# Order of TensorE in a two-layer decoder trunk: narrow instructions take turns with wide products

## The chip, the cores and the metric

The kernel runs on one core of a Trainium2 chip. The metric is the device time of one execution, in microseconds; a row of the profile is one instruction, or a run of equal ones, of that execution. Besides the engine for products (TensorE, PE in the rows, with its loads of weights shown apart as PEld) the core has VectorE (DVE), ScalarE (ACT), GpSimd (POOL) and SyncE (SP, which issues the transfers).

## The reference, cut to what matters

A trunk of two layers on x (512 tokens, width 1024). Layer 0 mixes by a gated delta rule (4 heads of 128) and by dilated window attention (8 heads of 64), layer 1 by a diagonal state-space model (S5) and a gated product; each layer then attends into 256 memory tokens and runs a SwiGLU of hidden width 2816. All in float32.

```python
def reference(x, mem, positions, ...):
    h = x
    for layer in range(DEPTH):
        i = layer // 2
        if layer % 2 == 0:
            mix = delta_dilated_mixer(h, positions, hyb_w_in[i], ..., hyb_w_out[i])
        else:
            mix = s5_mixer(h, s5_a_re[i], ..., s5_glu_wo[i], s5_glu_wg[i])
        h = post_norm(h, mix, ln_mix_g[layer], ln_mix_b[layer])
        h = post_norm(h, memory_cross_attention(h, mem, ...), ln_x_g[layer], ln_x_b[layer])
        h = post_norm(h, swiglu(h, ffn_wg[layer], ffn_wu[layer], ffn_wd[layer]), ...)
    return h

    # inside the delta rule: chunks in order, each needs the state of the one before
    def step(state, inp):
        q_c, w_c, u_c, k_c, a_c, gl = inp
        v_new = u_c - einsum(w_c, state)
        out = einsum(q_c, state) + einsum(a_c, v_new)
        state = state * exp(gl) + einsum(k_c, v_new)
        return state, out
```

## The kernel before

**Products.** Every float32 product with weights is made from three: both operands are split into a high and a low part (tiles `hi` and `lo`, made by ScalarE and VectorE from `raw`, into which the weights are loaded), and high times high, high times low and low times high are added up in one bank of the accumulator (`ps`, 8 banks). Such a product moves 512 or 256 columns past a 128x128 tile of weights; these are called *wide* below. The *narrow* instructions are transposes (128x128, `ident` in the row) and products of unsplit float32 tiles: 128x128 in the delta rule, 64x64 and 32x32 in the inverse of its triangular matrices.

**Recording and planning.** The program doesn't issue as it goes. Each operation is recorded by the class `Order` with its cost (`cost`) and its predecessors; its number in the record (moved a little for weights and tables) is its priority. `Order.order` then simulates the engines. Whenever an engine is free it takes the ready operation with the lowest number whose tiles can be had, looking past at most `TRIES` (40) others. The cost of each operation and fixed delays between engines set when the next is ready, so the plan of one engine depends on the costs of all. `issue` writes the instructions out in the order found, each engine's own queue in program order; hence nearly all rows carry one line, L439 (several instructions recorded as one: L437). Since the plan fills an engine's gaps with what is ready, wide products of the next part of the program are found between the steps of a chain.

**The first mixer, where the prediction looks.** In the order of the record: the input projection of the delta rule with its convolution; on VectorE the solve of 31 triangular rows (tiles `big_119` and `t2_184`, two operations a row, the next row needing the one before); the gate of z (`z_sink`, which writes `big_68` from `t2_205` to `t2_208`); the solved rows go out to memory and come back, are masked (`t2_210` to `t2_216`, by `masks`), transposed (into `ps_211` to `ps_217`, **T287** below, after the second number in `ps_211_287`), and inverses are put together from 32x32 and 64x64 pieces (banks `ps_218` to `ps_233`). Then the delta rule, four chunks of 128 tokens in a chain. A step is called by the second number of its bank: F316 and F318 (state and output of the first chunk), **F325** (the key times the state), F327, F333, **T324** (transposes of the chunk's output), **F329** and F331 (the next state), F339, F341, F347, T338, F343, and so on to **T402**, transposes for the attention. Between two products of this chain VectorE or ScalarE read the bank and write the next operand. The wide products that fill are the projections for the attention: V into `ps_292` and `ps_293`, and the keys or queries for the rotation into `ps_308_384` and `ps_309_385` (24 wide products each). Behind that come the window attention, its output product (`ps_612` and others), whose operands are transposed first (`ps_627`, `ps_628`), cross-attention and the FFN.

Of the kernel before, what the change touches and what calls it, by code (L numbers as in the profile page):

```python
# [33 lines left out]
TRIES = 40  # L34
FILL = 1
PRE = 1
GATE = 5
STEPS = (4, 2)
LATER = 100
FFN_PARTS = ((0, 6), (6, 11))  # L40
# [64 lines left out]
class Order:  # L105
# [173 lines left out]
    def scratch(self, ap):  # L279
        self.hist.setdefault(ap.tensor.name, ([], []))  # L280


    def order(self, seq, prio):
        ops = self.ops
# [35 lines left out]
        sched = [False] * n  # L320
        dma_free = 0.0
        slow = 3.4
        out = []
        for op in ops:
            if npred[op.i] == 0:
# [2 lines left out]
        while len(out) < n:  # L328
# [5 lines left out]
            for e in self.eng:  # L334
                if busy[e] > now + 1e-9:
                    nxt.append(busy[e])
                    continue
                skipped, got = [], None
                tries = 0
                while heaps[e]:  # L340
                    item = heapq.heappop(heaps[e])
                    op = ops[item[1]]
                    if sched[op.i]:
                        continue
                    ok = True
                    need = {}
                    for t in op.tiles:
                        if t in live or t not in self.tags:
                            continue
                        tag, b = self.tags[t]  # L350
                        need[tag] = need.get(tag, 0) + 1
                        if sum(x <= now + 1e-9 for x in free[tag]) < need[tag]:
                            if free[tag]:
                                nxt.append(min(free[tag]))
                            ok = False
                            break
                        f = first[t]
                        if tag in KEEP and len(free[tag]) <= KEEP[tag][0] and rank[t] > rank_at[tag][head] + KEEP[tag][1]:
                            ok = False
                            break  # L360
                        if f > head and prof[tag][head:f].max(initial=0) >= b:
                            ok = False
                            break
                    if ok:
                        got = op
                        break
                    skipped.append(item)
                    tries += 1
                    if tries > TRIES:
                        break  # L370
                for it in skipped:
                    heapq.heappush(heaps[e], it)
                if got is None:
                    continue
                op = got
                a = next(x for x in op.alts if x[0] == e)
                for t in op.tiles:
                    if t in self.tags and t not in live:
                        tag, b = self.tags[t]
                        live.add(t)  # L380
                        free[tag].sort()
                        free[tag].pop(0)
                        if first[t] > head:
                            prof[tag][head:first[t]] += 1
                sched[op.i] = True
                op.engine = e
                op.start = now
                if e == "sp":
                    busy[e] = now + a[4]
                    nbytes = max(_bytes(x) for x in op.outs + op.ins)  # L390
                    s = max(now + 1.65, dma_free)
                    dma_free = s + nbytes / 3.6e5
                    op.done = dma_free + 0.75
                else:
                    cost = a[4]
                    if e == "pe":
                        if now - busy[e] > 3.4:
                            slow = now + 3.4
                        cost += min(cost, max(slow - now, 0.0) * 0.5)
                    busy[e] = now + cost  # L400
                    op.done = busy[e]
                nxt.append(busy[e])
                out.append((op, a))
                for t in op.tiles:
                    if t in self.tags:
                        end[t] = max(end.get(t, 0.0), op.done)
                        left[t] -= 1
                        if left[t] == 0:
                            tag, b = self.tags[t]
                            free[tag].append(end[t] + self.LAT)  # L410
                            prof[tag][head:last[t] + 1] -= 1
                for s in op.succ:
                    npred[s.i] -= 1
                    when[s.i] = max(when[s.i], op.done + self.LATS.get((e, s.alts[0][0]), self.LAT))
                    if npred[s.i] == 0:
                        heapq.heappush(pend, (when[s.i], s.i))
                while head < n and sched[seq[head].i]:
                    head += 1
# [23 lines left out]
def _size(ap):  # L442
    n = 1
    for _, c in list(ap.ap)[1:]:
        n *= c
    return n
# [1268 lines left out]
```

## Time and profile before

| | us |
|---|---|
| runs of the kernel | 1540.59, 1544.35, 1544.91 |
| median | 1544.35 |
| the profiled execution | 1543.56 |
| span of its records | 1541.8 |
| TensorE busy within the span | 1508.7 |
| VectorE, ScalarE, GpSimd busy | 984.9, 552.5, 57.0 |

The profile shows one execution. The span runs from the first record to the last; 1.8 us of the execution lie around it. A timeline row tells when a run of equal instructions started and how long it lasted; matmuls overlap, so what one costs is read from the start of one row to the start of the next. In brackets stands the time in which the engine had nothing to do just before, and the engine whose result ended it.

### The profile page before, as it was taken

Reading aid. Unit: us, or ns where it says so; the run is one execution under the profiler, and the core shown is the slowest. Engines: PE = TensorE matmul, PEld = TensorE weight load, DVE = VectorE, ACT = ScalarE, POOL = GpSimd, SP = SyncE. Lnnn points to the kernel's source line nnn. Section 1 sums busy time; section 2 is a strip of 40 time slices with the busy share of each in tenths; the row PEclk is TensorE's granted clock in tenths of the full one; section 3 lists DMA queues with packets and bytes.
Section 4 is the critical chain, followed back from the end, with each engine's and each line's share of the span. In section 5 each row is a group of like instructions: output and inputs, shape, how many; then the busy total and the mean of one; then the engine's idle time right before and its main releaser. Section 6 shows DMA issues by size and latency. Waiting matters only on the chain.

```text
span 1541.8 us, 21120 instructions
## 1 busy us (share of the span) xinstructions
PE 1508.7 (98%) x8220; PEld 1268.3 (82%) x8220; DVE 984.9 (64%) x1880; ACT 552.5 (36%) x1008; POOL 57.0 (4%) x97
## 2 busy tenths in 40 slices
PE   7999899999999999999999899999999999999998
PEld 5888788689889887888888898888889888888886
DVE  6986576697557888626845899647557444234436
ACT  5533346544523354324341333323423222122311
POOL 1100000010100000010000000000000000000000
PEclk9999999999999999999999999999999999999999
DMA  6424134235223355445562652333212333233322
GB/s 201 115 57 123 47 119 137 64 98 163 62 76 116 110 192 176 150 165 174 186 220 76 245 191 86 128 110 121 65 57 82 109 99 102 85 110 96 96 69 96
DMA packets 125396, 184.01 MB, mean 119 GB/s; under 512 B 14128, under 2 KB 84656, under 8 KB 121200
## 3 DMA queue, kind: packets, MB, share of 16 engines
q1 hardware_dynamic: 125296, 182.66, 37.6%
q8 instruction: 65, 1.06, 0.3%
q14 instruction: 35, 0.29, 0.1%
HBM read 162.45 MB, written 20.19 MB: 118 GB/s over the span
## 4 chain that ended last, share of the span: by engine, by line
PE 88%; DVE 7%; DMA 2%; ACT 1%; issue 1%; SPq 0%; POOL 0%; DVEq 0%; ACTq 0%; POOLq 0%
PE ps L439 86%; DVE t L439 4%; DVE big L439 2%; PE ps L437 2%; DVE lo L439 1%; DMA raw<-in_hyb_w_in_dram 1%; DVE tiny L439 0%; DMA big<-s5m 0%; ACT big L439 0%; DMA raw<-in_xo_w_dram 0%; ACT hi L439 0%; ACT t L439 0%; DMA posi<-in_pos_t_dram 0%; SPq L439 0%; ACT L439 0%
## 5 line engine op out<-in xcount | busy, mean ns | idle before, releaser
L439 PE MATMUL ps<-big,hi 128*128 128x512 f32 (+1 forms) x2368 | 649.5, 360 | 6.1 <-ACT hi L439 4.5
L439 PE MATMUL ps<-hi,big 128*128 128x512 f32 x1728 | 548.2, 394 | 0.7 <-ACT big L439 0.4
L439 PEld LDWEIGHTS ps<-big,hi 128*128 128x128 f32 x2368 | 420.7, 190 | 72.4 <-ACT hi L439 4.7
L439 ACT ACTIVATE hi<-raw 128x1024 fp32r<-128x1024 f32 (+2 forms) x252 | 263.5, 1046 | 513.7 <-PE ps L439 355.7
L439 DVE TENSOR_TENSOR lo<-raw,hi 128x1024 fp32r<-128x1024 f32 (+2 forms) x252 | 303.4, 1205 | 224.8 <-ACT hi L439 221.4
L439 PE MATMUL ps<-big,lo 128*128 128x512 f32 (+1 forms) x1184 | 423.7, 359 | 2.5 <-DVE lo L439 2.5
L439 PEld LDWEIGHTS ps<-hi,big 128*128 128x128 f32 x1728 | 322.6, 188 | 66.4 <-DVE big L439 0.9
L439 PE MATMUL ps<-lo,big 128*128 128x512 f32 x864 | 338.3, 393 | 1.0 <-DVE lo L439 1.0
L439 PEld LDWEIGHTS ps<-big,lo 128*128 128x128 f32 x1184 | 224.6, 190 | 34.5 <-DVE lo L439 2.9
L439 PEld LDWEIGHTS ps<-lo,big 128*128 128x128 f32 x864 | 162.4, 188 | 35.5 <-DVE lo L439 2.2
L439 ACT ACTIVATE big<-ps 128x256 fp32r<-128x256 f32 (+2 forms) x188 | 89.4, 508 | 211.1 <-PE ps L439 202.0
L439 ACT ACTIVATE t<-ps 128x512 f32<-128x512 f32 (+6 forms) x147 | 68.8, 485 | 147.7 <-PE ps L439 139.0
L439 DVE TENSOR_TENSOR big<-ps,big 128x256 fp32r<-128x256 f32 (+1 forms) x152 | 77.6, 541 | 56.9 <-ACT big L439 54.7
L439 DVE SCALAR_TENSOR_TENSOR big<-big,ps 128x512 f32<-128x512 f32 x56 | 38.4, 685 | 86.7 <-PE ps L439 86.7
L439 DVE SCALAR_TENSOR_TENSOR t<-t,ps 128x512 f32<-128x512 f32 x72 | 49.0, 682 | 68.5 <-ACT t L439 49.8
L439 ACT ACTIVATE big<-t 32x128 f32<-32x128 f32 (+2 forms) x148 | 64.9, 455 | 24.3 <-DVE t L439 19.9
L439 DVE SCALAR_TENSOR_TENSOR big<-big,tiny,t 128x512 f32<-128x512 f32 x96 | 66.6, 745 | 0.0
L439 PE MATMUL ps<-ident,t 128*128 128x128 f32 x344 | 62.7, 275 | 3.4 <-ACT t L439 1.8
L439 POOL TENSOR_TENSOR tiny<-tiny,mhalf 128x1 f32<-128x1 f32 (+1 forms) x28 | 23.1, 825 | 962.3 <-DVE tiny L439 953.6
L439 PEld LDWEIGHTS ps<-ident,t 128*128 128x128 f32 x344 | 42.5, 140 | 15.6 <-ACT t L439 5.1
L439 PE MATMUL ps<-big,big 128*128 128x256 f32 (+2 forms) x328 | 54.9, 314 | 0.0
L439 PEld LDWEIGHTS ps<-big,big 128*128 128x128 f32 x328 | 47.8, 190 | 5.0
(145 smaller groups left out, 929.4 us busy)
## 6 DMA issues: line engine op xcount, KB each, us to landing
raw<-in_ffn_wg_dram SPq DMA_DIRECT2D x44, 512.0 KB, 3.8
raw<-in_ffn_wu_dram SPq DMA_DIRECT2D x44, 512.0 KB, 3.6
raw<-in_ffn_wd_dram SPq DMA_DIRECT2D x44, 512.0 KB, 4.1
s5m<-big SPq DMA_DIRECT2D x16, 1024.0 KB, 4.2
big<-s5m SPq DMA_DIRECT2D x16, 1024.0 KB, 6.3
raw<-in_hyb_w_in_dram SPq DMA_DIRECT2D x26, 512.0 KB, 3.8
raw<-in_xk_w_dram SPq DMA_DIRECT2D x16, 512.0 KB, 3.6
raw<-in_xv_w_dram SPq DMA_DIRECT2D x16, 512.0 KB, 4.1
```

Source lines behind the costliest of these rows:

```text
L437: op.inst = getattr(self.eng[e], f)(*a, **k)
L439: op.inst = getattr(self.eng[e], fn)(*args, **kw)
```

## The change

The planner gets two numbers, `WIDE` and `REACH`, and a function that sorts TensorE's operations into narrow and wide ones. When the last operation planned for TensorE was narrow, another narrow one that is ready is passed over in favour of a wide one that is ready and recorded at most 100 behind the first narrow one passed over; up to 200 operations are looked past for that. If there is none, the narrow one is taken as before. In the planner's account a narrow operation right behind a wide one costs 0.08 us less. No instruction is added or removed on any engine; since the plan's times change, VectorE, ScalarE and SyncE are written in another order too.

```diff
--- before.py
+++ after.py
@@ -35,6 +35,8 @@
 FILL = 1
 PRE = 1
 GATE = 5
+WIDE = 200
+REACH = 100
 STEPS = (4, 2)
 LATER = 100
 FFN_PARTS = ((0, 6), (6, 11))
@@ -279,6 +281,16 @@
     def scratch(self, ap):
         self.hist.setdefault(ap.tensor.name, ([], []))
 
+    @staticmethod
+    def kind(op):
+
+        _, fn, args, kw, _ = op.alts[0]
+        if fn == "transpose":
+            return "narrow"
+        if fn == "matmul":
+            return "wide" if args[1].dtype == F32R and _size(op.outs[0]) >= 256 else "narrow"
+        return fn
+
 
     def order(self, seq, prio):
         ops = self.ops
@@ -320,6 +332,7 @@
         sched = [False] * n
         dma_free = 0.0
         slow = 3.4
+        after = None
         out = []
         for op in ops:
             if npred[op.i] == 0:
@@ -335,7 +348,7 @@
                 if busy[e] > now + 1e-9:
                     nxt.append(busy[e])
                     continue
-                skipped, got = [], None
+                skipped, got, narrow = [], None, None
                 tries = 0
                 while heaps[e]:
                     item = heapq.heappop(heaps[e])
@@ -361,15 +374,19 @@
                         if f > head and prof[tag][head:f].max(initial=0) >= b:
                             ok = False
                             break
+                    if ok and e == "pe" and after == "narrow" and (self.kind(op) != "wide" or narrow is not None and prio[op.i] > prio[narrow.i] + REACH):
+                        narrow = narrow or op
+                        ok = False
                     if ok:
                         got = op
                         break
                     skipped.append(item)
                     tries += 1
-                    if tries > TRIES:
+                    if tries > (TRIES if narrow is None else WIDE):
                         break
                 for it in skipped:
                     heapq.heappush(heaps[e], it)
+                got = got or narrow
                 if got is None:
                     continue
                 op = got
@@ -394,6 +411,10 @@
                 else:
                     cost = a[4]
                     if e == "pe":
+                        kind = self.kind(op)
+                        if kind == "narrow" and after == "wide":
+                            cost -= 0.08
+                        after = kind
                         if now - busy[e] > 3.4:
                             slow = now + 3.4
                         cost += min(cost, max(slow - now, 0.0) * 0.5)
```

The first place is on TensorE, in front of the output product of the first mixer (`ps_612`), where its operands are transposed (`ident`). Before:

```order
L439 MATMUL ps_612_688<-hi_618_694,big_235_311 128x512
L439 MATMUL ps_627_703<-ident_1_72,big_580_656 128x128 x4
L439 MATMUL ps_612_688<-hi_618_694,big_235_311 128x512
L439 MATMUL ps_628_704<-ident_1_72,big_580_656 128x128 x4
L439 MATMUL ps_612_688<-lo_619_695,big_235_311 128x512
```

and now:

```order
L460 MATMUL ps_612_688<-lo_616_692,big_234_310 128x512
L460 MATMUL ps_627_703<-ident_1_72,big_580_656 128x128
L460 MATMUL ps_612_688<-hi_615_691,big_234_310 128x512
L460 MATMUL ps_627_703<-ident_1_72,big_580_656 128x128
L460 MATMUL ps_612_688<-hi_618_694,big_235_311 128x512
L460 MATMUL ps_627_703<-ident_1_72,big_580_656 128x128
L460 MATMUL ps_612_688<-lo_619_695,big_235_311 128x512
L460 MATMUL ps_627_703<-ident_1_72,big_580_656 128x128
```

The four transposes into one bank stood together; now a wide product stands between each two.

The second place is on TensorE, where the delta chain begins (transposes into `ps_211`, from the masked rows `t2_210`). Before:

```order
L439 MATMUL ps_293_369<-lo_305_381,big_9_80 128x512
L439 MATMUL ps_293_369<-hi_304_380,big_9_80 128x512
L439 MATMUL ps_308_384<-hi_313_389,big_6_77 128x512
L439 MATMUL ps_308_384<-lo_314_390,big_6_77 128x512
L439 MATMUL ps_308_384<-hi_313_389,big_6_77 128x512 x2
L439 MATMUL ps_211_287<-ident_1_72,t2_210_286 128x128 x4
L439 MATMUL ps_213_289<-ident_1_72,t2_212_288 128x128 x4
L437 MATMUL ps_218_294<-t2_210_286,big_98_172 32x32 x8
```

and now:

```order
L460 MATMUL ps_308_384<-hi_316_392,big_7_78 128x512 x2
L460 MATMUL ps_308_384<-lo_317_393,big_7_78 128x512
L460 MATMUL ps_308_384<-hi_316_392,big_7_78 128x512
L460 MATMUL ps_309_385<-hi_313_389,big_6_77 128x512
L460 MATMUL ps_309_385<-lo_314_390,big_6_77 128x512
L460 MATMUL ps_309_385<-hi_313_389,big_6_77 128x512 x2
L460 MATMUL ps_309_385<-lo_314_390,big_6_77 128x512
L460 MATMUL ps_309_385<-hi_313_389,big_6_77 128x512
L460 MATMUL ps_211_287<-ident_1_72,t2_210_286 128x128 x4
L458 MATMUL ps_218_294<-t2_210_286,big_98_172 32x32 x8
```

Before, four wide products into `ps_308` (an x2 counts two) stand between the last one into `ps_293` and these transposes; now twelve into `ps_308` and six into `ps_309` do, of which the last twelve are shown. VectorE, whose triangular solve must end before, reads there, around the last gate of z (`t2_208`), before:

```order
L439 SCALAR_TENSOR_TENSOR t2_208_284<-t2_208_284,ps_192_268 128x512
L439 TENSOR_TENSOR big_119_195<-big_119_195,t2_184_260 64x13x19
L439 SCALAR_TENSOR_TENSOR big_68_142<-t2_208_284,normg_29_101 128x512
L439 TENSOR_TENSOR t2_184_260<-big_119_195 64x240
L439 TENSOR_TENSOR big_119_195<-big_119_195,t2_184_260 64x12x20
```

and now:

```order
L460 SCALAR_TENSOR_TENSOR t2_208_284<-t2_208_284,ps_192_268 128x512
L460 TENSOR_TENSOR big_119_195<-big_119_195,t2_184_260 64x17x15
L460 SCALAR_TENSOR_TENSOR big_68_142<-t2_208_284,normg_29_101 128x512
L460 TENSOR_TENSOR t2_184_260<-big_119_195 64x256
L460 TENSOR_TENSOR big_119_195<-big_119_195,t2_184_260 64x16x16
```

The gate stood behind the row of 13 by 19 and now stands ahead of the row of 16 by 16: eight operations more of the solve come behind it.

The third place is on TensorE in the delta chain, from F327 (`ps_251`) to F329 (`ps_253`). Before:

```order
L439 MATMUL ps_248_324<-ident_1_72,t2_247_323 128x128
L439 MATMUL ps_309_385<-hi_319_395,big_8_79 128x512
L439 MATMUL ps_248_324<-ident_1_72,t2_247_323 128x128
L439 MATMUL ps_309_385<-lo_320_396,big_8_79 128x512
L439 MATMUL ps_248_324<-ident_1_72,t2_247_323 128x128 x2
L439 MATMUL ps_309_385<-hi_319_395,big_8_79 128x512 x2
L439 MATMUL ps_309_385<-lo_320_396,big_8_79 128x512
L439 MATMUL ps_309_385<-hi_319_395,big_8_79 128x512
L439 MATMUL ps_309_385<-hi_322_398,big_9_80 128x512
L439 MATMUL ps_309_385<-lo_323_399,big_9_80 128x512
L439 MATMUL ps_309_385<-hi_322_398,big_9_80 128x512
L439 MATMUL ps_253_329<-t2_252_328,big_25_97 128x128 x4
```

and now:

```order
L460 MATMUL ps_240_316<-t2_239_315,big_25_97 128x128 x4
L460 MATMUL ps_242_318<-t2_239_315,big_99_173 128x128 x4
L460 MATMUL ps_309_385<-lo_323_399,big_9_80 128x512
L460 MATMUL ps_249_325<-t2_241_317,big_66_140 128x128 x4
L460 MATMUL ps_309_385<-hi_322_398,big_9_80 128x512
L460 MATMUL ps_251_327<-t2_250_326,big_119_195 128x128 x4
L460 MATMUL ps_257_333<-t2_241_317,big_65_139 128x128 x4
L460 MATMUL ps_248_324<-ident_1_72,t2_247_323 128x128 x4
L460 MATMUL ps_253_329<-t2_252_328,big_25_97 128x128 x4
L460 MATMUL ps_255_331<-t2_252_328,big_99_173 128x128 x4
```

The wide products into `ps_309` between the steps are gone but for two, and the chain's steps follow each other.

## Rows read from the trace of the kernel before

**Rows 1.** The page: busy us of each engine (share of the span), instructions.

```profile
PE 1508.7 (98%) x8220; PEld 1268.3 (82%) x8220; DVE 984.9 (64%) x1880; ACT 552.5 (36%) x1008; POOL 57.0 (4%) x97
```

**Rows 2.** Stretches (us from:to): length, busy per engine (instructions), granted clock, DMA share, GB/s.

```profile
143.80:168.90 25.10, 25.03 (x365) 21.48 (x364) 9.66 (x24) 13.03 (x34) 1.01 (x1) 1.00 0.26 75
168.90:182.20 13.30, 7.83 (x49) 5.91 (x48) 7.27 (x25) 3.51 (x12) 1.01 (x1) 1.00 0.00 0
182.20:191.00 8.80, 8.80 (x55) 8.42 (x56) 7.38 (x25) 5.07 (x15) 1.37 (x1) 0.81 0.37 124
...
280.80:299.00 18.20, 16.35 (x133) 10.95 (x131) 12.08 (x34) 11.78 (x25) 0.00 (x0) 1.00 0.18 45
...
858.00:874.00 16.00, 11.20 (x86) 10.39 (x85) 14.48 (x21) 4.70 (x7) 0.10 (x1) 0.94 0.63 237
```

**Rows 3.** TensorE's timeline, transposes between wide products: start, us, instruction, count [idle <-releaser].

```profile
166.65 0.48 PE L439 MATMUL ps<-hi,big 128*128 128x512 f32 x1
166.97 0.27 PE L439 MATMUL ps<-ident,t 128*128 128x128 f32 x1
166.99 0.48 PE L439 MATMUL ps<-lo,big 128*128 128x512 f32 x1
...
187.47 0.60 PE L439 MATMUL ps<-ident,t 128*128 128x128 f32 x4
187.83 0.47 PE L439 MATMUL ps<-hi,big 128*128 128x512 f32 x1
188.14 0.39 PE L439 MATMUL ps<-lo,big 128*128 128x512 f32 x1
188.37 0.39 PE L439 MATMUL ps<-hi,big 128*128 128x512 f32 x1
```

**Rows 4.** TensorE's timeline, 64x64 pieces between wide products.

```profile
152.40 0.39 PE L439 MATMUL ps<-hi,big 128*128 128x512 f32 x1
152.72 0.68 PE L439 MATMUL ps<-t,big 64*64 64x64 f32 x8
153.32 0.50 PE L439 MATMUL ps<-hi,big 128*128 128x512 f32 x1
153.67 0.39 PE L439 MATMUL ps<-lo,big 128*128 128x512 f32 x1
```

**Rows 5.** TensorE's waits, 143 to 191: waits for: us in total, times, longest us.

```profile
PE ps L439 <- DVE big L439: 3.1, 2, 2.3
PE ps L439 <- DVE t L439: 1.7, 3, 0.7
PE ps L439 <- ACT t L439: 0.7, 1, 0.7
```

**Rows 6.** TensorE's timeline in the delta chain.

```profile
143.80 1.03 PE L439 MATMUL ps<-ident,t 128*128 128x128 f32 x8
...
165.04 1.05 PE L439 MATMUL ps<-t,big 128*128 128x128 f32 x8
165.84 0.47 PE L439 MATMUL ps<-hi,big 128*128 128x512 f32 x1
...
170.10 1.13 PE L439 MATMUL ps<-t,big 128*128 128x128 f32 x8 [0.77 <-DVE big L439]
...
182.20 5.44 PE L439 MATMUL ps<-t,big 128*128 128x128 f32 x32 [2.34 <-DVE big L439]
```

**Rows 7.** VectorE's timeline: a step of the triangular solve, and the masked rows.

```profile
123.50 0.39 DVE L439 TENSOR_TENSOR t<-big 64x240 f32<-64x240 f32 x1
...
124.36 0.39 DVE L439 TENSOR_TENSOR t<-big 64x231 f32<-64x231 f32 x1
...
142.61 0.68 DVE L439 TENSOR_TENSOR t<-t,masks 128x512 f32<-128x512 f32 x1
```

**Rows 8.** TensorE's timeline at the end of the window attention.

```profile
284.72 0.66 PE L439 MATMUL ps<-ident,t 128*128 128x128 f32 x4 [1.28 <-ACT t L439]
285.95 0.66 PE L439 MATMUL ps<-ident,t 128*128 128x128 f32 x4 [0.57 <-ACT t L439]
```

## The prediction

> **What bounds the kernel now.** I read the page first: TensorE is busy for 1508.7 of the 1541.8 us span, 98%, and VectorE, the next, for 984.9 [rows 1]. So the time is TensorE's own work plus about 33 us in which it waits or has no record, and a change of order can do two things: alter what a TensorE instruction costs next to its neighbours, and alter those waits. The table by stage comes second, to see where the waits are [rows 2]. The delta rule of the first mixer (168.9 to 182.2 us) leaves TensorE busy for 7.83 of 13.30 us; in the next stretch the granted clock averages 0.81; the end of the window attention (280.8 to 299) leaves out 1.85 us and the start of S5 4.80. Third, the timeline of TensorE where narrow instructions stand between wide ones, for the price of a neighbour [rows 3, 4], and last the waits and steps of the delta chain [rows 5, 6].
>
> **A narrow instruction behind a wide one.** The planner now believes that this saves 0.08 us. In the trace a wide product follows a wide one after 0.23 us (188.14 to 188.37) [rows 3]. A lump of four transposes takes 0.36 us to the next wide product (187.47 to 187.83), and that product needs 0.31 instead of 0.23 until the next starts: (0.36 + 0.31 - 0.23) / 4 = 0.11 us for each transpose. One transpose alone: from the wide product ahead of it to the wide product behind it 0.34 us (166.65 to 166.99), 0.34 - 0.23 = 0.11 [rows 3]. The transpose does start the next wide product 0.02 us after itself, as the planner was taught, but a wide product behind one stands for 0.32 instead of 0.23 (166.65 to 166.97), and the pair costs the same as in a lump. Counted over both programs' orders, the runs of narrow instructions between wide products grow from 243 to 434, those of length one from 89 to 320. At two decimals the rows give 0.00 +- 0.02 us for a new break; I take +0.01, so 191 x 0.01 = **+1.9 us**, ends 0 and +3.8. The 64x64 pieces are dearer: a lump of eight takes 0.60 us (152.72 to 153.32), but the product ahead stands for 0.32 and the one behind for 0.35 instead of 0.23 [rows 4], so a new break between such pieces costs (0.32 + 0.35 - 2 x 0.23) = 0.21 us.
>
> The Trainium skill, page "TensorE: Matmul & The Clock Gate", section "Step-by-step: what each phase is for", says that TensorE pulls the next load of weights ahead of products in flight, so that weights are loaded while the tile before is still computed. By that rule alone alternation should hide each transpose's load under a wide product, and the sum would be the second rival's. The trace agrees for the narrow instruction (0.02 us to the next start) and not for the wide one behind it (0.32 instead of 0.23), whose own load has only a short instruction to hide under.
>
> **Start of the delta chain.** The chain begins with the transposes T287 (8 of them at 143.80), which before start right behind wide products, without idle [rows 6]. In the order of before four products into ps_384 stand between the last one into ps_369 and T287; now there are eighteen, twelve into ps_384 and six into ps_385, because a wide product up to 100 records behind goes first: 14 x 0.23 = **+3.2 us** for T287. VectorE agrees from its side: eight more operations of the triangular solve stand behind the last gate of z (big_68 from t2_208), 32 instead of 24; one step of two takes 0.86 us there (123.50 to 124.36), 4 x 0.86 = 3.4 us; T287's input, which needs that solve, is begun at 142.61 [rows 7]. So T287's data is about as late as its turn: 147.0 to 147.2 instead of 143.80, and neither of the two repairs the other.
>
> **T287 to F314.** Wide products between them grow from 17 to 23: 6 x 0.23 = 1.4 us, and about four more breaks between 64x64 pieces, 4 x 0.21 = 0.8 us. TensorE has no idle time between 143.8 and 168.9 (25.03 of the 25.10 us up to 168.90 are busy [rows 2]), so nothing hides this: **+2.2 us**, low end 0 if these pieces wait for VectorE or ScalarE behind the shown products anyhow.
>
> **F325 to T402.** Before, 21 wide products into ps_385 stand between the steps of the chain; now one does. The other 20 are the 14 and the 6 of the two terms above, done ahead of these steps. That is 20 x 0.23 = 4.6 us of cover. In before, the chain already waits 3.1 + 1.7 + 0.7 = 5.5 us in spite of it, for VectorE and ScalarE [rows 5]: each step is a product, an operation on one of those engines, and the next product. I take it that where a wide product stood a wait of the same size stands now: the chain is no shorter, **0 us**, with -0.3 for the places where a wide product held a step up by part of its 0.23 us. The other end, every one of them only in the way, is -4.6 us.
>
> **The end of the attention.** Two transposes of the mixer's last heads wait 1.28 and 0.57 us for ScalarE [rows 8]. Two wide products (0.46 us) stand between the score products ahead of them and the scores behind; now none does, while other wide products move further back. **+0.6 us**, ends 0 and +1.5. Everywhere else (the FFN's order with the S5 tables is the same row for row, S5 and the second layer nearly so) I take 0, with 1.5 us either way.
>
> **The clock.** The 32 products from 182.20 on took 5.27 us to the next transposes, in a stretch with clock 0.81, behind the longest wait, 2.34 us [rows 2, 6]. At full clock eight take 0.80 us (165.04 to 165.84), 32 would take 3.2 [rows 6]. So this one dip costs 2.1 us. With fewer wide products in the chain it can begin earlier or come twice: 0 in the sum, +2.1 as the high end.
>
> **Sum.** Against the profiled run, 1543.56 us (its span of 1541.8 and 1.8 around it; the median of the runs is 1544.35): +1.9 + 3.2 + 2.2 - 0.3 + 0.6 = +7.6, so 1551.2, told as **1551 us**. A measurement of this kernel can tell 0.3%, 4.6 us, from no change, so all up to 1549 counts as the same.
>
> **Rivals.**
> *The chain gets shorter as its wide products leave.* TensorE's work is then moved, not uncovered, and the only losses are breaks: 1551.2 - 4.6 = about 1547 us, not slower by this measure. For it: from 143.8 to 168.9 TensorE never idles, so there the chain's steps could have been ready and held up by wide products. Against it: seven in a row stand ahead of F329, which waits 0.77 us for VectorE all the same (170.10 [rows 6]), so ahead of it they covered a wait. It decides if more than half of the 4.6 us were in the way (2.2 us less puts the time at 1549).
> *The credit is real.* A narrow instruction behind a wide one saves 0.08 us as planned: 191 x 0.08 = 15.3 us, less the losses of the chain and the attention, 5.7: 1534 us. It is the rule of the page named above of the Trainium skill, taken to its end. Against it stand the 0.31 and 0.32 of [rows 3].
> *The plan comes apart.* The planner thinks TensorE some 15 us faster in sum than it is (191 x 0.08), and orders VectorE and ScalarE by that; the waits at the start of S5 (4.80 us [rows 2]) then double, and the chain has a second dip of clock: 1551.2 + 4.8 + 2.1 = 1558 us. Against it: at the start of S5 VectorE's order has hardly moved.
> That the change does nothing can be left out: the orders differ as it says.
>
> **How the numbers follow.** The forecast has 0.62, with its own range from 1547.5 to 1555; I give 0.12 of it to times under 1549. The shorter chain has 0.20, the credit 0.05, the plan that comes apart 0.13. Slower: 0.50 + 0.13 = 0.63. Same: 0.12 + 0.20 = 0.32. Faster: 0.05. The range from 1545 to 1557 holds nearly all of the first (0.62), most of the second (0.15) and the near part of the last (0.05): 0.82.
>
> **What would show it.** Right: a wide product behind a single transpose still stands for 0.31 us or more; T287 starts near 147.1; TensorE's idle time in the delta chain grows from 5.5 us to about 10, under the same releasers; the two waits of the attention come to 2.5 or more instead of 1.85; the FFN takes as long as before. Wrong: idle time in the chain stays near 5.5 (the second case), TensorE's busy time falls by over 5 us (the credit), or S5's first waits exceed 6 us.

## The result, and the profile after

The changed kernel takes **1562.47 us** in the median (1561.84 to 1564.82) against 1543.17 of the kernel before: ratio 1.0129, 95% interval 1.011 to 1.0149. The forecast was 1551 with a range from 1545 to 1557: the sign was right, the loss was more than twice as large as forecast. The profiled execution took 1564.82 us, 21.3 more than that of before.

The page's line of busy times, to be held against [rows 1]:

```profile
PE 1520.6 (97%) x8220; PEld 1271.3 (81%) x8220; DVE 983.6 (63%) x1880; ACT 553.8 (35%) x1008; POOL 59.8 (4%) x97
```

The span grew from 1541.8 to 1563.0. TensorE's time that is not busy grew from 33.1 to 42.4 us (+9.3) and its busy time by 11.9, with the same 8220 instructions. The busy time has two parts. The granted clock stood at half for 10.2 us within TensorE's work before and for 30.7 now; less the idle time in these stretches (0.4 and 2.9), half of it is lost: (30.7 - 2.9) / 2 - (10.2 - 0.4) / 2 = **+9.0**. What is left, 11.9 - 9.0 = **2.9 us**, has no row of its own; the breaks between narrow and wide instructions would be in it.

Where it went shows in stretches cut at the same places of the program: the delta rule (last product into ps_369 to the last T402), the end of the attention, S5 with the gated product. Columns as in [rows 2]. Before:

```profile
142.70:187.80 45.10, 39.56 (x453) 33.84 (x452) 23.15 (x64) 20.41 (x59) 2.01 (x2) 0.96 0.16 47
280.80:297.80 17.00, 15.15 (x116) 10.09 (x114) 11.81 (x33) 10.88 (x25) 0.00 (x0) 1.00 0.14 38
864.30:988.80 124.50, 119.04 (x783) 106.52 (x782) 113.05 (x159) 41.36 (x59) 2.64 (x25) 0.99 0.47 151
```

and after:

```profile
142.30:195.60 53.30, 45.00 (x457) 37.87 (x457) 23.75 (x68) 20.79 (x59) 2.01 (x2) 0.87 0.18 49
288.90:307.70 18.80, 15.21 (x107) 9.30 (x107) 10.60 (x32) 10.92 (x25) 0.00 (x0) 0.91 0.13 35
877.10:1008.70 131.60, 122.81 (x785) 108.81 (x784) 113.85 (x160) 41.73 (x61) 2.60 (x25) 0.96 0.42 144
```

Length less the first number behind it is TensorE's idle time: 5.5 to 8.3 in the delta rule, 1.9 to 3.6 in the attention, 5.5 to 8.8 in S5; the clock (third column from the right) fell in all three, from 0.96 to 0.87, 1.00 to 0.91, 0.99 to 0.96. The three stretches hold 8.2 + 1.8 + 7.1 = 17.1 of the 21.3 us. They don't hold quite the same instructions: after has four and two of TensorE's more in the first and third, nine fewer in the second.

The waits in the delta chain, to be held against [rows 5]:

```profile
PE ps L460 <- DVE big L460: 4.7, 2, 2.3
PE ps L460 <- DVE t L460: 2.9, 4, 1.2
PE ps L460 <- ACT t L460: 0.7, 1, 0.7
```

and TensorE's timeline there, to be held against [rows 6]:

```profile
146.66 0.60 PE L460 MATMUL ps<-ident,t 128*128 128x128 f32 x4
...
164.84 1.95 PE L460 MATMUL ps<-t,big 128*128 128x128 f32 x16
...
166.85 1.05 PE L460 MATMUL ps<-t,big 128*128 128x128 f32 x8
...
171.49 1.02 PE L460 MATMUL ps<-ident,t 128*128 128x128 f32 x4 [0.91 <-DVE t L460]
174.85 1.43 PE L460 MATMUL ps<-t,big 128*128 128x128 f32 x8 [2.34 <-DVE big L460]
177.49 2.07 PE L460 MATMUL ps<-t,big 128*128 128x128 f32 x8 [1.21 <-DVE t L460]
180.25 2.07 PE L460 MATMUL ps<-t,big 128*128 128x128 f32 x8 [0.69 <-ACT t L460]
182.76 3.48 PE L460 MATMUL ps<-t,big 128*128 128x128 f32 x16 [0.44 <-DVE t L460]
...
189.07 5.44 PE L460 MATMUL ps<-t,big 128*128 128x128 f32 x32 [2.33 <-DVE big L460]
```

T287 starts at 146.66 instead of 143.80. F329 (174.85) waits 2.34 us where it waited 0.77, and behind it (177.49) eight products take 2.07 us where eight took 1.05 at full clock [rows 6]: the clock is at half from 175.5 to 185.8, and again from 189.2 to 192.6. The same alternation as in [rows 3], now the usual picture:

```profile
194.58 0.27 PE L460 MATMUL ps<-ident,t 128*128 128x128 f32 x1
194.61 0.48 PE L460 MATMUL ps<-lo,big 128*128 128x512 f32 x1
194.93 0.27 PE L460 MATMUL ps<-ident,t 128*128 128x128 f32 x1
194.95 0.48 PE L460 MATMUL ps<-hi,big 128*128 128x512 f32 x1
```

A wide product still stands for 0.32 us behind a transpose (194.61 to 194.93), and the transpose for 0.02 to 0.03.

### The profile page after: what moved, and what is told of

The parts are those of the page before. It is cut to its first block, busy times and chain, and to the rows that moved or that the text cites. A ratio compares the mean times of both kernels' runs of the same rounds, so it can differ in the third digit from the quotient of the medians.

```text
span 1563.0 us, 21116 instructions
## 1 busy us (share of the span) xinstructions
PE 1520.6 (97%) x8220; PEld 1271.3 (81%) x8220; DVE 983.6 (63%) x1880; ACT 553.8 (35%) x1008; POOL 59.8 (4%) x97
## 3 DMA queue, kind: packets, MB, share of 16 engines
q8 instruction: 64, 1.05, 0.3%
## 4 chain that ended last, share of the span: by engine, by line
PE 91%; DVE 5%; DMA 2%; ACT 1%; issue 1%; SPq 0%; POOL 0%; DVEq 0%; ACTq 0%; POOLq 0%
PE ps L460 89%; DVE t L460 2%; PE ps L458 2%; DVE big L460 1%; DVE lo L460 1%; DMA raw<-in_hyb_w_in_dram 1%; ACT big L460 0%; DMA big<-s5m 0%; DMA raw<-in_xo_w_dram 0%; ACT t L460 0%; ACT hi L460 0%; DMA t<-in_x_t_dram 0%; DVE tiny L460 0%; DMA posi<-in_pos_t_dram 0%; SPq L460 0%
## 5 line engine op out<-in xcount | busy, mean ns | idle before, releaser
L460 PE MATMUL ps<-big,hi 128*128 128x512 f32 (+1 forms) x2368 | 656.9, 363 | 5.6 <-ACT hi L460 4.9
L460 PE MATMUL ps<-hi,big 128*128 128x512 f32 x1728 | 555.4, 398 | 1.6 <-ACT big L460 1.5
L460 PE MATMUL ps<-lo,big 128*128 128x512 f32 x864 | 343.6, 399 | 1.4 <-DVE lo L460 1.4
L460 PEld LDWEIGHTS ps<-big,lo 128*128 128x128 f32 x1184 | 225.1, 190 | 34.1 <-DVE lo L460 1.5
L460 DVE SCALAR_TENSOR_TENSOR big<-big,ps 128x512 f32<-128x512 f32 x56 | 38.1, 681 | 84.1 <-PE ps L460 84.0
L460 PE MATMUL ps<-ident,t 128*128 128x128 f32 x344 | 75.4, 275 | 5.0 <-ACT t L460 3.5
```

Source lines behind the costliest of these rows:

```text
L460: op.inst = getattr(self.eng[e], fn)(*args, **kw)
```

## The experiments

The theory after the traces (A): stages lose the wide products that covered their waits, the longer waits take the clock with them, and neither the turns as such (B) nor the planner's credit (C) costs much alone. Diffs are against the changed kernel unless said otherwise. In the table, *idle* is the profiled span less TensorE's busy time, *half clock* the time at half clock within TensorE's work, from its first rise to full on, both of the one profiled execution. That one need not be typical: e5's is 10.5 us quicker than e5's median, e9's 8.6 slower than e9's. Half clock differs without a change of order, too: the first 36 us have 3.4 us of it in before and 6.8 in e7 and e15, whose order on TensorE is that of before.

| kernel | median us | ratio to before (95%) | idle | half clock |
|---|---|---|---|---|
| before | 1543 to 1545 | | 33.1 | 10.2 |
| after | 1562.5 | 1.0129 (1.0110 to 1.0149) | 42.4 | 30.7 |
| e1, turns, no credit | 1557.7 | 1.0085 (1.0053 to 1.0117) | 38.7 | 20.5 |
| e2, credit, no turns | 1556.0 | 1.0071 (1.0047 to 1.0095) | 38.1 | 20.5 |
| e3, not in the first mixer | 1549.8 | 1.0036 (1.0022 to 1.0050) | 37.2 | 10.2 |
| e4, only in the first mixer | 1559.4 | 1.0097 (1.0082 to 1.0112) | 40.6 | 30.7 |
| e5, both halves, no turns | 1555.9 | 1.0083 (1.0057 to 1.0109) | 34.4 | 10.2 |
| e6, turns, both halves | 1548.8 | 1.0036 (1.0023 to 1.0048) | 32.9 | 17.1 |
| e7, before, longer wait | 1549.0 | 1.0041 (1.0022 to 1.0060) | 34.5 | 13.7 |
| e8, split behind the scan | 1560.8 | 1.0109 (1.0088 to 1.0129) | 42.6 | 17.1 |
| e9, e6 in the mixer only | 1550.9 | 1.0046 (1.0026 to 1.0066) | 36.2 | 34.1 |
| e10, e5 in the mixer only | 1547.3 | 1.0025 (1.0012 to 1.0037) | 34.5 | 10.2 |
| e11, scan and scaling first | 1561.8 | 1.0105 (1.0086 to 1.0124) | 39.7 | 30.7 |
| e12, e5 again | 1547.9 | 1.0035 (1.0019 to 1.0051) | 33.4 | 13.7 |
| e13, turns of transposes only | 1561.4 | 1.0104 (1.0088 to 1.0119) | 41.5 | 30.7 |
| e14, e13 with both halves | 1547.1 | 1.0016 (1.0006 to 1.0025) | 32.7 | 17.1 |
| e15, before, scans first | 1543.9 | 0.9994 (0.9984 to 1.0005) | 31.4 | 10.2 |

**The two parts, each alone.** e1:

```diff
-                        if kind == "narrow" and after == "wide":
-                            cost -= 0.08
```

> The turns are kept, the 0.08 us credit in the planner's account is taken out. In its order the delta chain keeps its wide products: none ahead of T287, 15 from T287 to F314, 30 from F325 to T402 (after: 18, 23, 2). Theory A (the loss sits in stages that lose their cover and then the clock, because the credit lets the planner draw wide products forward): near the kernel before, 1544 to 1549 us, half-clock time back near 10 us. Theory B (turns as such are dear, by breaks between narrow and wide): 460 runs of narrow instructions, more than the 434 of after, so 1560 to 1566 us. Theory C (the credit alone misleads the planner): 1543 to 1547.

e2:

```diff
-                    if ok and e == "pe" and after == "narrow" and (...):
+                    if ok and e == "pe" and after == "turns off" and (...):
```

> The credit is kept, the turns are taken out: 248 runs of narrow instructions as in before (243), the chain's wide products nearly as before (4, 19, 19). Theory A: 1541 to 1547 us, since neither the chain nor the breaks change. Theory B: as before, 1541 to 1546. Theory C: most of the loss stays, 1555 to 1564.

Both miss theory A. Either part alone loses 11 to 13 us. e2 does so with hardly more breaks than before, and as C said of it, so the credit alone is enough for some 60% of after's 19.3 us; but e1, without the credit, is far from C's 1543 to 1547. e1 has more breaks than after and loses less, short of B's 1560 to 1566 in the median (two of its four executions are inside); that breaks (B) are not the price shows in e6 below, with 470 runs of narrow instructions and 4.8 us. What A said of the delta chain held: with the wide products in place e1 idles 4.9 us there (before 5.5, after 8.3). The rest of e1 and e2 is idle time and clock in other stages: S5 with the gated product idles 7.9 and 8.5 us (before 5.5).

**By place.** An operation remembers whether it was recorded in the first mixer, and both parts ask it (e3 leaves them out there, e4 elsewhere):

```diff
-                    if ok and e == "pe" and after == "narrow" and (...):
+                    if ok and e == "pe" and after == "narrow" and op.turns and (...):
...
-                        if kind == "narrow" and after == "wide":
+                        if kind == "narrow" and after == "wide" and op.turns:
```

> Turns and credit only for operations recorded behind the first mixer; its own order is that of before. From the traces, after loses 7.3 us up to 189 (delta chain), 3.3 up to 291 (attention) and some 10 behind. Theory A: those 10.6 us come back, 1550 to 1555 us, with half-clock time in S5 and behind only. Theory B: breaks go in proportion, 351 of 434 runs, (351-243)/(434-243) = 57% of the loss stays, 1552 to 1555; A and B part by the stages here, not by the sum.

> Turns and credit only for operations recorded up to the end of the first mixer, the rest as before. Theory A: the 10.6 us of delta chain and attention stay, and what lies behind goes: 1553 to 1556 us, T287 near 146.7, half-clock time of some 17 us up to 300. Theory B: (349-243)/(434-243) = 55% of the loss, 1552 to 1555, but spread over the breaks and without more half-clock time.

e3 lost 5.3 us: delta rule and attention are those of before to 0.02 us, S5 idles 8.9 us. e4 lost 14.8: the delta rule is 8.0 us longer, 2.8 of it idle, T287 is late as in after, and half-clock time is 30.7 us; S5 idles 5.5 as before. That is more than A or B gave e4 (at most 1556 us, measured 1559.4), and e3 lies just under their ranges. So the stages lose by themselves, each where the new plan reaches, and the mixer has about three quarters of the loss.

**The planner's account.** The rows say that what a narrow instruction saves behind a wide one, the wide one behind it gives back. e6 charges that too; e5 is the same without turns:

```diff
                         if kind == "narrow" and after == "wide":
                             cost -= 0.08
+                        elif kind == "wide" and after == "narrow":
+                            cost += 0.08
```

> Turns as in the change (470 runs of narrow instructions), with both halves of the account. The delta chain keeps its wide products (0 ahead of T287, 15 to F314, 29 or 30 behind F325). Theory D: the breaks are left, 227 x 0.01 = 2.3 us, and little else, 1545 to 1549 us. Theory E: 1551 to 1559 us, like the turns without credit.

> No turns; the planner credits 0.08 us to a narrow operation behind a wide one and charges 0.08 to a wide one behind a narrow one, as the rows have it. Theory D (half an account makes the plan run ahead of TensorE, so VectorE and ScalarE are queued for moments that come later): with both halves the plan is at least as true as before, 1539 to 1546 us. Theory E (the order of before is a good draw, and any other plan of the same quality costs 5 to 12 us): 1549 to 1557 us, as with the credit alone.

With turns and both halves (e6) the loss shrinks from 19.3 to 4.8 us and the idle time is 32.9, no more than before, at 470 runs of narrow instructions: this is what theory D (half an account makes the plan run ahead of TensorE) asked for, and not what E (any other plan costs 5 to 12 us) did. e5 came out the other way: its median of 1555.9 lies in E's range (1549 to 1557) and nearly 10 us above D's (1539 to 1546). Its profiled execution idles 34.4 us, near before too, but that is the quickest of the five, and they spread from 1545.4 to 1558.9 us with mean clocks from 0.996 to 0.987. Once more the same kernel:

> The account with both halves and no turns, everywhere, once more: its executions lay at 1545.4 (mean clock 0.996, profiled) and at 1555 to 1559 (0.987 to 0.989). If the difference is the clock alone: a profile of an execution of the second sort has the same order and about the same idle time (26 to 28 us) and some 20 to 28 us more at half clock; it shows where they start. If this one too is of the first sort, nothing is told.

This time the profiled execution was again among the quickest (1546.1, clock 0.994), and the median 1547.9: the same kernel lost 11.8 us in the median of five executions and 3.8 in that of eight, and its time goes with the mean clock. So D and E stay undecided. No execution of this kernel with the lower clock was profiled; one of e9 was. e9 and e10 are e6 and e5 with the account (and the turns) in the first mixer only:

> Turns and both halves of the account (0.08 credited and charged), for operations of the first mixer only; behind it the planner is that of before. In the profile of the turns with both costs everywhere, TensorE idled 1.2 us less than before in the delta chain and 1.3 less at the end of the attention, and 2.0 more in S5. If the gain in the mixer is real and S5's loss belongs to the new plan there: 1539 to 1543 us, delta chain with 4.3 us of idle time, S5 with 5.5 as before. If S5's plan suffers from what reaches it out of the mixer: 1544 to 1548.

> As the last, without turns: only the account, both halves, and only in the first mixer. If the turns bring nothing of their own, within 2 us of the last, 1539 to 1544 us. The account without turns everywhere had one execution at 1545.4 and four at 1555 to 1559 with a lower mean clock (0.996 against 0.987 to 0.989); if that clock loss starts in the mixer it is here too, 1550 to 1556.

S5 idles 5.5 us in both, as before, so the loss there belongs to the plan made there. Both were expected to beat before (1539 to 1543 or 1544 us), and neither does: 1550.9 and 1547.3. e9's profiled execution took 1559.55 us, others of it 1547; its stretches where the inverse's small pieces run:

```profile
147.20:151.60 4.40, 3.52 (x127) 2.85 (x127) 2.24 (x3) 2.06 (x3) 0.00 (x0) 1.00 0.31 114
151.60:168.70 17.10, 17.05 (x101) 13.66 (x101) 3.06 (x6) 4.68 (x14) 0.00 (x0) 0.50 0.23 62
```

and the row between them on TensorE:

```profile
151.66 0.42 PE L462 MATMUL ps<-t,big 32*32 32x32 f32 x8 [0.93 <-issue]
```

Behind a run of 32x32 pieces and a pause of 0.93 us the clock is at half for 17.1 us in which TensorE is busy throughout, with 0.05 us of idle time in it. Half of that, 8.5 us, is two thirds of the spread of this kernel (12.7). That the quicker executions don't have this dip isn't shown, since none of them was profiled.

**What a wait costs in clock.** In the kernel before, order kept, two VectorE operations on which F329 waits are issued three times:

```diff
-                op.inst = getattr(self.eng[e], fn)(*args, **kw)
+                for _ in range(1 + op.again):
+                    op.inst = getattr(self.eng[e], fn)(*args, **kw)
```

> The kernel before, order kept on every engine; only the two VectorE operations that split the first chunk's output (about 0.54 us each, F329 waits for the second) are issued three times each. F329's wait of 0.77 us becomes about 2.9. If idle time is all that counts: +2.1 to +2.2 us in the chain. If a wait of that length also lowers the granted clock, as behind 2.34 us in before and in after: a stretch at half clock within 6 us behind F329, of 3.4 us or more, in which the chain's products need twice as long: +3.5 to +5 us by the T402 transposes.

TensorE's timeline and the stretches around it:

```profile
170.89 0.39 PE L442 MATMUL ps<-hi,big 128*128 128x512 f32 x1
174.56 2.04 PE L442 MATMUL ps<-t,big 128*128 128x128 f32 x8 [3.28 <-DVE big L442]
176.25 0.77 PE L442 MATMUL ps<-hi,big 128*128 128x512 f32 x1
176.82 0.63 PE L442 MATMUL ps<-lo,big 128*128 128x512 f32 x1
```

```profile
170.90:174.50 3.60, 0.38 (x2) 0.00 (x0) 3.37 (x6) 0.00 (x0) 0.00 (x0) 0.95 0.00 0
174.50:177.50 3.00, 2.94 (x11) 2.54 (x11) 0.86 (x4) 0.00 (x0) 0.00 (x0) 0.50 0.00 0
```

The wait is 3.28 us instead of 0.77, and the products behind it run at half clock, eight in 2.04 us instead of 1.13. The delta rule is 3.4 us longer, just under the 3.5 to 5 expected with a dip: 2.5 of wait and 0.9 of what the dip adds (at half clock from 174.1 to 177.5, some 1.5 us of work, part of which is made up in the waits behind). So a longer wait alone, with the order of TensorE kept, had a dip behind it. How long the dip lasts is another matter: 3.4 us here, where three wide products still stand between F329 and F331, and 10.2 us in all five profiles in which F329 waits 2.3 us and none stands there (after, e4, e8, e11, e13). No run varies these two apart. And the wait does not settle it: the start of S5 has the same order and the same longest wait of TensorE, 2.06 us, in before, e7 and e15, with a dip behind it in before only. In this order:

```profile
864.00:876.00 12.00, 8.49 (x57) 7.89 (x57) 12.00 (x18) 2.12 (x2) 0.10 (x1) 0.86 0.46 150
869.00:881.00 12.00, 8.51 (x69) 7.89 (x68) 11.91 (x16) 2.94 (x5) 0.10 (x1) 1.00 0.49 169
865.00:877.00 12.00, 8.51 (x68) 7.90 (x68) 11.88 (x16) 2.97 (x5) 0.10 (x1) 1.00 0.49 168
```

The whole kernel lost 5.0 us in the median. The profiled execution lost 4.2; 2.0 of it stand in the first 36 us, in which nothing was changed, and are not the experiment's; on the other side the dip that before has at the start of S5 is missing.

**VectorE's queue at the end of the attention.** T619 and T623, called by their banks as the steps of the chain are, are the two transposes of [rows 8]. In after T619 waits 3.21 us, where it waited 1.28. First the two splits ahead of the first score scan were put behind it (e8), then also behind the scaling of its maximum (e11), both in the list that is issued:

```diff
+        scan = next(x for x in self.issued[at:] if ... "tensor_tensor_reduce")
+        for x in late:
+            self.issued.remove(x)
+        at = self.issued.index(scan) + 1
+        self.issued[at:at] = late              # e8
+        self.issued[at:at] = [mx] + late       # e11
```

> The changed kernel, with two VectorE operations put back to where before has them: the split of the attention's third row of blocks behind the first scan of scores of the fourth row instead of ahead of it (in after they hold the queue from 290.1 to 291.8, 2.4 us behind the first scores). If that order makes the 3.2 us wait of the transposes T619: the wait falls to 1.0 to 1.5 us, the half-clock stretch behind it (295.0 to 298.4 in after) goes, and the kernel is 2 to 4 us faster than after, 1558 to 1560.5. If the wait has another cause, no change.

> The changed kernel with VectorE's queue as before at the first score scan of the attention's last row of blocks: scan, its maximum scaled, and only then the two splits (with the splits behind the scan but ahead of the scaling, T619's wait had fallen from 3.21 only to 2.60 us, since ScalarE's exponential needs the scaled maximum). If this is the cause: the first exponential starts within 0.3 us behind the scaling, T619 waits 0.8 to 1.3 us. The half-clock stretch behind it (3.4 us, worth 1.7) goes if the shorter wait spares it. Whole kernel 1557 to 1560 us.

e8 brought the wait to 2.60 only, and the dip behind it stayed. In after VectorE, ScalarE and TensorE (third column) read:

```profile
290.83 1.10 DVE L460 TENSOR_TENSOR big<-t,big 128x256 fp32r<-128x256 f32 x2 [0.71 <-ACT big L460]
291.84 0.69 DVE L460 CUSTOM_DVE_ANT_0 t<-ps,big 128x512 f32<-128x512 f32 x1
...
293.25 0.72 ACT L460 ACTIVATE t<-t,tiny 128x512 f32<-128x512 f32 x1 [1.99 <-DVE tiny L460]
...
294.12 0.66 PE L460 MATMUL ps<-ident,t 128*128 128x128 f32 x4 [3.21 <-ACT t L460]
```

and in e11:

```profile
291.81 0.69 DVE L472 CUSTOM_DVE_ANT_0 t<-ps,big 128x512 f32<-128x512 f32 x1
...
292.54 0.15 DVE L472 TENSOR_SCALAR tiny<-tiny 128x1 f32<-128x1 f32 x1
292.62 1.10 DVE L472 TENSOR_TENSOR big<-t,big 128x256 fp32r<-128x256 f32 x2
...
292.78 0.68 ACT L472 ACTIVATE t<-t,tiny 128x512 f32<-128x512 f32 x1
...
293.61 0.66 PE L472 MATMUL ps<-ident,t 128*128 128x128 f32 x4 [0.97 <-ACT t L472]
```

In after the splits hold VectorE's queue for ScalarE (0.71) and for themselves (1.0), and the scan and its scaling stand behind. With scan and scaling first the wait is 0.97, the exponential starts 0.24 us behind the scaling's start, the clock stays at full there, and this end of the attention takes 3.1 us less (15.7 instead of 18.8). Over the whole kernel, forecast at 1557 to 1560, 0.7 us against after cannot be told from nothing: its executions ran from 1556.7 to 1564.2, and the profiled one has 6.8 us at half clock in its first 36 us where after has 3.4, which hides the dip that is gone. The same edit in the kernel before (e15, with the first two scans ahead of the splits):

> The kernel before with VectorE's queue changed at one place: the first two score scans of the attention's last row of blocks, each with its maximum scaled at once, and the two splits behind them instead of between. If scan and scaling gate T619 and T623 in before too, their waits of 1.28 and 0.57 us fall to about 0.4 each and the end of the attention is 0.8 to 1.3 us shorter; the whole kernel 1542.5 to 1544, which a comparison can hardly tell from before.

The idle time at this place falls by 1.1 us, and the whole is 0.9994 (0.9984 to 1.0005): unclear, and the only version that is not slower than before.

**Turns of a chain's products.** In after the products of an S5 step take turns too, and the step then waits. From TensorE's timeline of after:

```profile
972.53 0.48 PE L460 MATMUL ps<-lo,big 128*128 128x512 f32 x1
972.84 0.38 PE L460 MATMUL ps<-big,t 128*128 128x128 f32 x2
972.98 0.48 PE L460 MATMUL ps<-hi,big 128*128 128x512 f32 x1
974.25 0.63 PE L460 MATMUL ps<-ident,big 128*128 128x128 f32 x4 [0.78 <-DVE t L460]
```

e13 passes over transposes only, e14 does so with both halves of the account:

```diff
-... after == "narrow" and (self.kind(op) != "wide" or ...)
+... after == "narrow" and op.alts[0][1] != "matmul" * (self.kind(op) == "narrow") and (self.kind(op) != "wide" or ...)
```

> The changed kernel, but only transposes wait for a wide product; float32 products (delta chain, its inverse, S5) are never passed over. The credit stays as it is. Theory F (turns hurt where a step of a chain waits for its turn, and the wide products that it lets by are the ones that would cover the wait behind it): in S5 the step's eight products stay together, and S5 with the gated product returns from 8.8 us of idle time to 5.5 to 6.5; the delta chain keeps 10 wide products behind F325 (after: 2) and loses part only; together 1551 to 1557 us. Theory G (any new plan idles more in S5, by its other queues): idle time there stays at 7.5 to 9 us, 1556 to 1561.

> As the last, with both halves of the account. The delta chain's wide products are as in before (4 ahead of T287, 17 to F314, 22 behind F325; with turns for all and both costs 0, 15, 30). Theory F: delta chain and S5 idle as in before (5.5 each, within 0.7), breaks (398-243) x 0.01 = 1.6 us: 1543 to 1547 us. Theory G: S5 idles 2 us more, 1546 to 1549.

e13's S5 idles 8.6 us, as much as after's, so the turns of its products are not what costs there as long as the credit stands (theory G); its waits between 950 and 990 are those of e2 (there between 940 and 985), one line in either:

```profile
PE ps L460 <- DVE t L460: 3.4, 3, 1.9
```

The delta chain kept 10 wide products and idled 7.0 us, between before and after. e14 idles 5.5 us in the delta rule and 5.1 in S5, the forecast of theory F, and is the best version with turns: 2.7 us slower than before, with no more idle time in all (32.7 against 33.1) and half clock of 17.1 instead of 10.2 us.

## Why the prediction was right in sign and wrong in size

The sum gave +7.6 us, the profiled executions differ by 21.3. Two steps of the prediction failed: "The clock ... 0 in the sum", and "Everywhere else ... I take 0", which had S5 and the second layer in it.

- **Breaks.** Not shown. 2.7 us were forecast with the 64x64 pieces (1.9 + 0.8), and 2.9 are left when idle time and clock are taken off, but the agreement may be luck: the same subtraction leaves 0.1 us in e1, with more breaks than after, 2.0 in e15, with the order of before on TensorE, and 5.7 in e8, with that of after.
- **Start of the chain, T287 to F314.** Right. T287 came 2.9 us later (3.2 forecast), and F316 5.0 us later (159.86 to 164.84), against 3.2 + 2.2 = 5.4. F316 and F325 in TensorE's timeline before:

```profile
159.86 1.95 PE L439 MATMUL ps<-t,big 128*128 128x128 f32 x16
...
161.87 1.05 PE L439 MATMUL ps<-t,big 128*128 128x128 f32 x8
```

- **F325 to T402.** Right up to the clock: F329 started 4.75 us later than before (170.10 to 174.85) and F325 4.98 (161.87 to 166.85), so this part of the chain, without 17 of its 18 wide products, was 0.2 us shorter (0.3 forecast), and the first rival (a chain that shortens) is out. Idle time grew to 8.3, not 10.
- **The clock.** This step failed: "0 in the sum, +2.1 as the high end". In TensorE's busy time it measured +9.0. The row with 5.44 us for 32 products was priced, but the waits that the forecast itself added were not followed to their clock: a dip of 10.2 us stands behind F329's wait, which went from 0.77 to 2.34 (e7 shows a dip behind a longer wait alone, though one of 3.4 us), and another behind the attention's, gone in e11. Not all of the 9.0 is time lost, since a product at half clock also fills part of a wait: from F329 to the first T402 the 10.2 us more at half clock made 2.4 us (187.47 - 170.10 = 17.37 before, 194.58 - 174.85 = 19.73 after, with one wide product of 0.32 more in it), so in this chain alone the clock cost about what the high end had.
- **The end of the attention.** The place was right, the size not: idle +1.7 instead of +0.6, and a dip of 3.4 us (1.7) on it. The wait came from VectorE's queue (e11), not only from the two wide products that left.
- **Elsewhere 0, 1.5 either way.** This step failed too, and by place it is half of the 13.7 us that the forecast lacks: S5 with the gated product lost 7.1 us, 3.3 idle and the rest mostly clock (6.8 us more at half). The 0 rested on VectorE's order at the start of S5, which had hardly moved; the time went between 880 and 980, in steps that were not compared. From the end of the attention to S5, cross-attention and FFN among it, 569.4 us were taken instead of 566.5. Which queue makes S5's waits stays open.
- **The rivals.** The credit as a real saving, the second, is out (0.32 us in the rows above). The third, "the plan comes apart" (0.13, 1558 us), was the nearest in time, but not by its own signs: idle time at the start of S5 did not double, it is 5.0 us where it was 4.8. That a planner which thinks TensorE faster than it is loses the time is not shown either. Of the kernels with half an account (after, e2, e3, e4, e8, e11, e13) all idle 37 to 43 us; with both halves (e5, e6, e10, e12, e14) 32.7 to 34.5, e9 36.2; before, with none, 33.1. That speaks for it, one execution of each; against it stand e5's median and e1, which has turns and no account at all, is as balanced as e6, and idles 38.7. So half an account lost time wherever it was tried, but a balanced one does not always save it; what sets e1 apart from e6 stays open, as does the queue that costs S5 its 2 to 3 us in e1, e5, e6 and e12 and not in e14.

## What to carry to other kernels

A gain that the profile shows at one instruction has to be looked for at its neighbours before it goes into a cost table: the transpose behind a wide product was 0.08 us cheaper, the wide product behind it 0.09 dearer. That a list scheduler which is told only the first half orders every queue for moments that come later was the theory here and is not shown: with both halves 4.8 us were lost (e6), 2.7 (e14), 11.8 and 3.8 (e5 and e12, the same kernel), without any account 13.1 (e1). In a chain that alternates between engines, wide products that stand between its steps cover waits; spent ahead of the chain they are gone, and waits that appear may be paid a second time at half clock, as behind 2.34 and 3.21 us in after. And 0 is a forecast like any other: half of the miss lay in a stage that was put at 0 after its start alone.

## What was not expected of the hardware

- The granted clock fell behind waits of 2.34 us (after, F329), 3.21 (after, T619) and 3.28 (e7), and stayed at full in e11 with a wait of 0.97 at T619's place. But it stayed at full in e10, too, with 2.74 us at that place (283 to 300 us: 1.00), and a wait of 2.06 us in one and the same order had a dip behind it in before and none in e7 and e15. So these waits are where dips were found, and their length alone did not decide.
- It also stayed at half with TensorE busy: in e9 for 17.1 us from the 32x32 pieces on, behind a pause of 0.93 us, in an execution of 1559.6 us, where the quickest of the same kernel took 1546.9.
- Two executions of one program can differ by 13 us (e5: 1545.4 and 1558.9) with mean clocks of 0.996 and 0.987. An estimate from these: 0.009 x 1557 = 14 us, so the clock is enough to explain it; the second execution was not profiled.
